# Early attention tasks in three lines with stores from ScalarE's queue, a reordered start of the output projection, and squares added in halves

## The chip, the cores and the metric

The kernel runs on one core of a Trainium2 chip. The metric is the device time of one execution, in microseconds (us); three runs of the kernel before gave 1561.88, 1563.29 and 1563.96, the median is 1563.29. The engines are named as in the profile: PE is the tensor engine, DVE VectorE, ACT ScalarE, POOL GpSimd, SP the engine that only issues DMAs here.

## The reference

One layer of a hybrid streaming encoder in fp32, on 1024 prompt rows and 32 sample rows (1056 columns in the kernel, where the activations lie transposed), with D_MODEL = 1024, eight heads of 64, a convolution branch of 512 channels and an MLP of 4096:

```python
h = rmsnorm(x, g_mix)
proj = h @ w_in                      # q, k, v, conv parts, two gates
y_attn = attend(q, k, v) @ w_attn_out
conv_out, new_buf = causal_conv(cc * cx, conv_buf, conv_w)
y_conv = (cb * conv_out) @ w_conv_out
merged = sigmoid(ga) * y_attn + sigmoid(gc) * y_conv
x = x + merged @ w_o
x = x + square(relu(rmsnorm(x, g_ffn) @ w_up)) @ w_down
x = x + sigmoid(rmsnorm(x, g_ple) @ w_ple_gate) * (p @ w_ple)
# attend: z = q k^T / 8, strictly causal;
# a = exp(log_sigmoid(z) + sum of log_sigmoid(-z) over the keys in between); out = a v
```

Outputs are the rms-normed rows, the keys and values, and the last rows of the convolution's input.

## The kernel before, in words

Every fp32 matmul is done as three matmuls on a high and a low part of each operand (a value is copied to a reduced type by ACT, and DVE subtracts that copy from the value for the low part). The large products are done as seven products of half-size blocks (Strassen-Winograd), with column quarters of 264; the halves and sums of blocks that this needs (B11, B21, B22, T1 to T4) are formed and split by ACT, DVE and POOL beside the matmuls.

The stages, with the times of the profile: the input projection to about 400 us; the attention loop to about 620; the branch products (`ps_oa`, `ps_oc`) to about 697; the output projection to about 780; up products to about 1120; down products to about 1448; then the per-layer embedding and the last norm.

**Attention.** 64 steps, each one tile of 128 queries of one head against all earlier keys. `ORDER` writes out what a step issues: the scores `z` (L864, L865) and their sigmoid `r` on ACT (L868; the score tile has one buffer, so PE's next `z` waits for the sigmoid before it), a running product by DVE (L882), turns of the weights by PE (`pa`, L918) with copies on ACT and DVE (L921, L922), and the weighted values `av` (L939). Between these, `fill` issues matmuls of other products in shares worked out ahead. SP's queue brings q, keys and values (L836 to L852), convolution data (L962) and weights. All engines work in order, so an instruction that waits holds whatever was issued behind it on its engine.

**The early tasks.** From step 3 on, one generator, `prior = ahead_all()`, is stepped once or twice per step (`1 + n % 2`, L1365). It does four gates and then eight weights one after the other. `ahead_gate` (L638) loads gate columns from `gd` (L640), three yields later scales them on DVE (`scaled`, L527), a yield later takes the sigmoid on ACT (L645) and stores to `gs_` (L646). `ahead_attn` (L627) loads a block of `w_attn_out` (L630), three yields later copies its high part on ACT (L633), takes the low part on DVE (L634) and stores both to `aod` (L635). Loads and stores all go through SP. The results are read back by the branch stage.

**The output projection.** `output_projection` (L1588) keeps a table of jobs, `at(q, f, ...)`: job f is issued at PE's unit q, a unit being 12 matmuls. The first jobs end the last branch output (`branch_post`, `merge_add`), form and split its halves (`merge_high` on ACT, `merge_low` on DVE, L1030 and L1034), sum them (`merge_sums`, L1054 to L1062) and split the parts T1 to T4 (`turn_part`, L1064, which also records at L1030 and L1034). `proj_high` (L1562) and `proj_low` (L1566) split the weights: `w0oA` (L1564) and `w1oA` (L1568). Results are added to `ceo` by DVE (L1682).

**The mean of squares.** `mean_squares` (L1716) is stepped once per unit in the up phase, from unit `SQ_AT` = 70 on. For each of eight tiles it loads (L1722), five yields later squares on ACT (L1725), a yield later adds on DVE (L1729); then three matmuls with ones (`ps_ms`, L1733) sum over the partitions. Meanwhile `mid_sums` (L1756) forms and stores the sums `m`, `ta`, `tb` of each set. Tiles come from one pool of 34 buffers.

Of the kernel before, what the change touches and what calls it, by code (L numbers as in the profile page):

```python
# [9 lines left out]
F32 = mybir.dt.float32  # L10
# [7 lines left out]
KD = D // P  # L18
# [25 lines left out]
CFILL = 4  # L44
ORDER = "LSAFBFG"
START = 2.5
SQ_AT = 70
MM = {mybir.EngineType.Activation, mybir.EngineType.PE, mybir.EngineType.DVE, mybir.EngineType.Pool}


# [1 line left out]
def tile_step(  # L52
# [574 lines left out]
    def ahead_attn(n):  # L627
        t = blk(f"ao{n}", F32R, [P, 2, 4, P])
        raw = t[:, 1].bitcast(F32)
        nc.sync.dma_start(raw, w_attn_out[n])  # L630
        for _ in range(3):
            yield
        nc.scalar.copy(t[:, 0], raw)  # L633
        dve(t[:, 1], raw, t[:, 0].bitcast(F32), op=sub)  # L634
        nc.sync.dma_start(aod[n], t.bitcast(F32).rearrange("p e k n -> p e (k n)"))  # L635
        yield

    def ahead_gate(n):  # L638
        m = blk(f"ga{n}")
        nc.sync.dma_start(m, gd[n])  # L640
        for _ in range(3):
            yield
        scaled(m)
        yield
        nc.scalar.activation(m, m, AF.Sigmoid)  # L645
        nc.sync.dma_start(gs_[n - 4], m)  # L646
        yield

    def ahead_all():
        for n in range(4, 8):  # L650
            yield from ahead_gate(n)
        for n in range(KD):
            yield from ahead_attn(n)

    def follow(nm, n, ms, wait=0):
        gens = []
# [366 lines left out]
    def merge_add(n, c):  # L1023
        dve(mg[n][:, c], mg[n][:, c], fetched["a", n][1][:, c], op=add)
# [111 lines left out]
    def branches():  # L1136

        seq = SEQ_B
        for i, b in enumerate(seq):
            prev, nxt = seq[i - 1] if i else None, seq[i + 1] if i + 1 < len(seq) else None  # L1140
            if i + 2 < len(seq):
                branch_fetch(seq[i + 2])
            else:
                row_fetch() if i + 2 == len(seq) else proj_fetch("A12", 1)
            done = prev and prev[0] == "a"
            if nxt:
                branch_high(nxt)
            else:
                row_high()
            branch_group(b, 0)  # L1150
            if prev:
                branch_post(prev, 2)
            if done:
                merge_add(prev[1], full[0])
                merge_high(prev[1])
            if nxt:
                if i:
                    branch_scale(nxt)
                branch_low(nxt)
                branch_sigmoid(nxt)  # L1160
            else:
                row_low()
                xload("ce", 0)
            if done:
                merge_low(prev[1])
                merge_sums(prev[1])
            for f in BESIDE.get(i, ()):
                f()
            branch_group(b, 1)
            branch_post(b, 0)  # L1170
            if nxt is None:
                merge_add(b[1], ts[0])
                proj_fetch("A12", 2)
            branch_group(b, 2)
            branch_post(b, 1)
            if nxt is None:
                merge_add(b[1], ts[1])
                merge_high(b[1], "1")
                merge_low(b[1], "1")
                proj_high("A12", 1)  # L1180
                proj_low("A12", 1)

    LK = PAST + DEC
    sampled = []
# [45 lines left out]
    with tc.manual_schedule(engines=MM):  # L1230
        nc.scalar.preload_act_table_set("sqrt_and_others")
        run(first_gates())
        for s_ in range(2, len(SETS)):
            nm, n = SETS[s_]
            if s_ == 2:
                side.append(after(1, stats_x()))
            elif s_ == 4:
                nc.scalar.preload_act_table_set("sigmoid_and_others")
            elif s_ == len(SETS) - 1:
                prior = ahead_all()  # L1240
            if s_ + 1 < len(SETS):
                side.append(prepare(f"i{s_ + 1}", AT_IN))
            else:
                side.extend([after(4, second_parts(0)), after(6, second_parts(1)), after(4, call(hooks_to, -20)), after(10, call(hooks_to, 0))])
            if s_ + 2 < len(SETS):
                side.append(after(5, call(fetch_in, s_ + 2)))
            m = blk(f"m1_i{s_}"), blk(f"m2_i{s_}")
            run(seven(f"i{s_}", *m, copy_of))
            if s_ + 1 < len(SETS):
                follow(nm, n, m, 6 * (s_ == 2))  # L1250
            else:
                last_m = n, m
        keys_values(0, 0)
        pools[:] = [gps]
        run(ahead(START))
        while side:
            run(range(1))
# [99 lines left out]
    with tc.manual_schedule(engines=MM):  # L1357
        queries(0, 0, 0)
        queries(0, 0, 1)
        for i, m in enumerate(last_m[1]):  # L1360
            nc.sync.dma_start(gd[last_m[0] + i], m)
        for n in range(LAST + 3):
            done_f, parts = 0, None
            if n > 2:
                for _ in range(1 + n % 2):  # L1365
                    next(prior, None)
            if n == 1:
                sample_loads()
            elif n == 3:
                sample_keys()  # L1370
            if n < LAST:
                i = steps[n][2]
                if i % 2 == 0 and n + 4 < LAST:
                    p_, j_, i_ = steps[n + 4]
                    queries(p_, j_, i_ // 2)
                if i == 2 and n + 8 < LAST:
                    keys_values(*steps[n + 8][:2])
            for op in ORDER:
                if op == "S" and n < LAST:
                    scores(*steps[n])  # L1380
                    if n == LAST - 1:
                        zf = zps.tile([P, 2, 512], F32, tag="z", name="zf")
                        spare_ps.extend(zf[:, h, :] for h in range(2))
                elif op == "L":
                    if 1 <= n <= LAST:
                        weigh(*steps[n - 1])
                    for f in pending + split_low:
                        f()
                    pending.clear()
                    split_low.clear()  # L1390
                elif op == "F" and n < LAST + 2:
                    done_f += 1
                    fill(share[n] + (share[n + 1] - share[n]) * done_f / nf)
                    if done_f == 1 and n in SAMPLE_AT:
                        next(sample, None)
                elif op == "G" and n >= 3 and steps[n - 3][2] % 2 == 1:
                    p, j, i_ = steps[n - 3]
                    gather(p, j, i_ // 2)
                elif op in "AB" and 2 <= n <= LAST + 1:
                    if op == "A":  # L1400
                        parts = flip(*steps[n - 2])
                    next(parts, None)
            for p, c in splits.get(n, ()):
                split_high(p, c)
            branches_ahead(n)
            if n == LAST + 1:
                fill(2 * total)
                hooks_to(len(plan))
                split_high(3, slice(0, 768))
        for f in pending + split_low:  # L1410
            f()
        split_high(3, slice(768, T))
        split_low.pop()()
# [174 lines left out]
    def output_projection():  # L1588
# [4 lines left out]
            jobs.setdefault(q, []).append(partial(f, *a))  # L1593

        last = KD - 1
        at(0, branch_post, ("a", last), 2)
        at(0, merge_add, last, ts[2])
        at(0, proj_fetch, "A12", 3)
        at(0, xload, "ce", 1)
        for j in (2, 3):  # L1600
# [7 lines left out]
        at(42, early_up, 1)  # L1608
        at(3, xload, "xb", 0)
        at(3, xload, "m2", 0)  # L1610
        at(1, merge_high, last, "2")
        for q, k, j in (
            (1, "T1", 0), (2, "T1", 1), (3, "T1", 2), (5, "T1", 3), (5, "T2", 0), (6, "T2", 1), (7, "T2", 2), (8, "T2", 3),
            (9, "T3", 0), (9, "T3", 1), (10, "T3", 2), (11, "T3", 3), (12, "T4", 0), (13, "T4", 1), (14, "T4", 2), (15, "T4", 3),
        ):
            at(q, turn_part, k, j)
        at(2, merge_low, last, "2")
        at(3, merge_sums, last, ("T3",))
        at(4, merge_sums, last, ("T2",))
        at(8, merge_sums, last, ("T4",))  # L1620
        for j in (1, 2, 3):
            q = AT["A11", j]
            for n in range(4):
# [92 lines left out]
    def mean_squares():  # L1716
# [3 lines left out]
        for n in range(KD):  # L1720
            r = blk(f"sq{n}")
            nc.sync.dma_start(r, xd[n])  # L1722
            for _ in range(5):
                yield
            nc.scalar.square(r, r)  # L1725
            yield
            ss = ss or r
            if n:
                dve(ss, ss, r, op=add)  # L1729
        rs2 = blk("rs2")  # L1730
        for c in ts:
            ps = tps.tile([P, 512], F32, tag="tp", name=f"ps_ms{c.start}")[:, :TT]
# [673 lines left out]
```

## Time and profile before

| | |
|---|---|
| median of three runs | 1563.29 us |
| the profiled execution | 1562.97 us |
| its span in the trace | 1561.2 us |
| PE busy | 1518.1 us, 97% of the span |
| DVE, ACT, POOL busy | 73%, 49%, 18% |
| mean granted clock of PE | 0.991 |
| bytes moved | 293.20 MB, 188 GB/s on the mean |

A row of a group gives line, engine, operation, output and inputs, the count and durations. A row of the timeline gives start and duration of one instruction, and in brackets the idle time of its engine before it and what released it. A row of waits gives who waited, for whom, the total, the number of times and the longest. PEclk is the share of its full clock that PE was granted. SPq and ACTq are the queues of DMA issues.

### The profile page before, as it was taken

The numbers are of one execution on the slowest core, as the hardware profiler recorded it, in microseconds if no ns is written. First come the engines' busy times: TensorE is split into PE (matmuls) and PEld (weight loads), VectorE is DVE, ScalarE is ACT, GpSimd is POOL, SyncE is SP. The second block draws the span as 40 slices with busy tenths as digits, with TensorE's granted clock in tenths as the row PEclk, the third lists the DMA queues.
The fourth block names the chain that finished last, engine by engine and source line by source line (L and its number), as shares of the span: only waits on it lengthen the run. The fifth ranks groups of instructions, "written<-read, shape, count | busy, mean of one in ns | idle before, by whom it ended". The sixth has DMA issues, their size and how long they took to land. (4 is left out here: it accounts for less than half of the span.)

```text
span 1561.2 us, 29913 instructions
## 1 busy us (share of the span) xinstructions
PE 1518.1 (97%) x11888; PEld 1501.3 (96%) x11888; DVE 1132.4 (73%) x1590; ACT 763.4 (49%) x1415; POOL 286.2 (18%) x318
## 2 busy tenths in 40 slices
PE   7999999999899899999999999999999999999997
PEld 7999999999798799999999999999999999999997
DVE  7568665667487788788876677755577995889756
ACT  6644444434466566224375555455644334444644
POOL 2223332221012222000001222222020130000253
PEclk9999999999999999999999999999999999999999
DMA  6513445414769852555754455443786897774443
GB/s 226 201 53 125 166 154 187 164 56 164 213 204 286 261 168 90 179 173 193 266 197 161 170 207 194 159 148 138 272 303 200 270 333 230 223 258 129 145 130 116
DMA packets 122765, 293.20 MB, mean 188 GB/s; under 512 B 14048, under 2 KB 34784, under 8 KB 122624
## 3 DMA queue, kind: packets, MB, share of 16 engines
q1 hardware_dynamic: 122336, 290.96, 55.6%
q8 instruction: 93, 1.52, 0.4%
q14 instruction: 48, 0.39, 0.1%
q10 hardware_dynamic: 288, 0.32, 0.1%
HBM read 204.15 MB, written 87.07 MB: 187 GB/s over the span
## 5 line engine op out<-in xcount | busy, mean ns | idle before, releaser
L1989 PE MATMUL ps_dn<-fh,whi_dn 128*128 128x264 f32 x896 | 255.0, 285 | 0.0
L1990 PE MATMUL ps_dn<-fl,whi_dn 128*128 128x264 f32 x896 | 254.8, 284 | 0.0
L1991 PE MATMUL ps_dn<-fh,wlo_dn 128*128 128x264 f32 x896 | 254.8, 284 | 0.0
L1991 PEld LDWEIGHTS ps_dn<-fh,wlo_dn 128*128 128x128 f32 x896 | 168.7, 188 | 0.1
L1990 PEld LDWEIGHTS ps_dn<-fl,whi_dn 128*128 128x128 f32 x896 | 168.6, 188 | 0.0
L1989 PEld LDWEIGHTS ps_dn<-fh,whi_dn 128*128 128x128 f32 x896 | 168.6, 188 | 0.0
L208 POOL TENSOR_TENSOR s_u<-raw_u,raw_u 128x512 f32<-128x512 f32 x22 | 32.7, 1487 | 367.2 <-DVE slS_u L169 317.0
L882 DVE TENSOR_TENSOR_SCAN r<-r 128x128 f32<-128x128 f32 (+3 forms) x64 | 86.6, 1353 | 3.4 <-POOL r L875 3.4
L208 POOL TENSOR_TENSOR s_i<-raw_i,raw_i 128x512 f32<-128x512 f32 x32 | 43.6, 1363 | 239.9 <-DVE slS_i L169 209.8
L1876 ACT CAST whi_dn<-raw_dn 128x1024 fp32r<-128x1024 f32 x40 | 42.0, 1050 | 83.0 <-PE ps_dn L1990 82.9
L1882 DVE TENSOR_TENSOR wlo_dn<-raw_dn,whi_dn 128x1024 fp32r<-128x1024 f32 x40 | 61.1, 1528 | 28.7 <-ACT whi_dn L1876 28.7
L241 PE MATMUL ps_A11i<-T,shS_i 128*128 128x264 f32 x256 | 73.1, 285 | 0.0
L875 POOL TENSOR_SCALAR_AFFINE_SELECT r<-r 128x128 f32<-128x128 f32 x64 | 35.4, 553 | 205.8 <-ACT r L868 198.2
L243 PE MATMUL ps_A11i<-T,slS_i 128*128 128x264 f32 x256 | 72.9, 285 | 0.0
L242 PE MATMUL ps_A11i<-T,shS_i 128*128 128x264 f32 x256 | 72.7, 284 | 0.0
L169 DVE TENSOR_TENSOR slS_i<-s_i,shS_i 128x512 fp32r<-128x512 f32 x48 | 34.9, 732 | 50.1 <-ACT shS_i L167 49.9
L1751 ACT ACTIVATE m<-m 128x528 f32<-128x528 f32 (+1 forms) x52 | 31.7, 610 | 80.2 <-DVE m L288 28.6
L1902 DVE TENSOR_TENSOR fl<-mr,fh 128x1056 fp32r<-128x1056 f32 x56 | 69.9, 1248 | 0.3 <-ACT q L1942 0.3
L922 DVE TENSOR_TENSOR at<-pa,at 128x512 fp32r<-128x512 f32 (+2 forms) x96 | 51.8, 549 | 22.4 <-ACT at L921 18.3
L2073 POOL TENSOR_TENSOR xx<-xx,pgs 128x384 f32<-128x384 f32 (+1 forms) x23 | 24.2, 1057 | 216.8 <-DVE pgs L2072 210.2
L1897 ACT CAST fh<-mr 128x1056 fp32r<-128x1056 f32 x56 | 60.0, 1072 | 0.2 <-issue 0.2
L169 DVE TENSOR_TENSOR slS_u<-s_u,shS_u 128x512 fp32r<-128x512 f32 x48 | 35.9, 747 | 33.1 <-ACT shS_u L167 33.1
(541 smaller groups left out, 5705.0 us busy)
## 6 DMA issues: line engine op xcount, KB each, us to landing
raw_dn<-in_w_down_dram SPq DMA_DIRECT2D x56, 512.0 KB, 4.8
raw_i<-in_w_in_dram SPq DMA_DIRECT2D x36, 512.0 KB, 4.4
mr<-mdT SPq DMA_DIRECT2D x32, 528.0 KB, 5.4
raw_u<-in_w_up_dram SPq DMA_DIRECT2D x32, 512.0 KB, 3.8
mr<-mdB SPq DMA_DIRECT2D x24, 528.0 KB, 6.3
mdB<-m SPq DMA_DIRECT2D x44, 264.0 KB, 2.7
raw_pg<-in_w_ple_gate_dram SPq DMA_DIRECT2D x17, 512.0 KB, 3.5
mdT<-ta SPq DMA_DIRECT2D x32, 264.0 KB, 2.1
```

Of the source, the lines that this page charges most:

```text
L169: dve(l, src, h.bitcast(F32), op=sub)
L208: f()
L241: nc.tensor.matmul(p_, wh[:, k, :], o[:, 0, c], start=new and n == 0, stop=False, **on)
L242: nc.tensor.matmul(p_, wh[:, k, :], o[:, 1, c], start=False, stop=False, **on)
L243: nc.tensor.matmul(p_, wl[:, k, :], o[:, 0, c], start=False, stop=z, **on)
L882: nc.vector.tensor_tensor_scan(rev, rev, rev, 1.0, ALU.mult, ALU.bypass)
L1882: dve(lo, raw, hi.bitcast(F32), op=sub)
L1897: nc.scalar.copy(h, mraw[v])
L1902: dve(l, mraw.pop(v), opd[v].bitcast(F32), op=sub)
L1989: nc.tensor.matmul(ps, hi[:, j, :], oh, start=j == 0, stop=False)
L1990: nc.tensor.matmul(ps, hi[:, j, :], ol, start=False, stop=False)
L1991: nc.tensor.matmul(ps, lo[:, j, :], oh, start=False, stop=j == NP_ - 1)
```

## The change

Three parts. First, the early tasks run in three lines, each stepped once per step of attention: weights 0 to 3, gates 4 to 7, weights 4 to 7, beginning at steps 3, 4 and 5. A load now comes five yields ahead of its use; the stores are issued by ACT, that of a weight two yields after its split. Second, in the table of the output projection, the parts of T1 come first and the last branch output later, and the weight split of the branch stage's end stands ahead of the halves. Third, the squares start at unit 40, each add is made in two halves of 528 columns with two yields ahead of each, and four yields follow the last.

```diff
-SQ_AT = 70
+SQ_AT = 40
...
     def ahead_attn(n):
...
         nc.sync.dma_start(raw, w_attn_out[n])
-        for _ in range(3):
+        for _ in range(5):
             yield
         nc.scalar.copy(t[:, 0], raw)
         dve(t[:, 1], raw, t[:, 0].bitcast(F32), op=sub)
-        nc.sync.dma_start(aod[n], t.bitcast(F32).rearrange("p e k n -> p e (k n)"))
+        yield
+        yield
+        nc.scalar.dma_start(aod[n], t.bitcast(F32).rearrange("p e k n -> p e (k n)"))
         yield
     def ahead_gate(n):
...
-        for _ in range(3):
+        for _ in range(5):
             yield
         scaled(m)
         yield
         nc.scalar.activation(m, m, AF.Sigmoid)
-        nc.sync.dma_start(gs_[n - 4], m)
-        yield
-
-    def ahead_all():
-        for n in range(4, 8):
-            yield from ahead_gate(n)
-        for n in range(KD):
-            yield from ahead_attn(n)
+        nc.scalar.dma_start(gs_[n - 4], m)
+        yield
+
+    def ahead_all(f, ns):
+        for n in ns:
+            yield from f(n)
...
                 merge_add(b[1], ts[1])
+                proj_high("A12", 1)
                 merge_high(b[1], "1")
+                proj_low("A12", 1)
                 merge_low(b[1], "1")
-                proj_high("A12", 1)
-                proj_low("A12", 1)
...
-                prior = ahead_all()
+                prior = [ahead_all(ahead_attn, (0, 1, 2, 3)), ahead_all(ahead_gate, (4, 5, 6, 7)), ahead_all(ahead_attn, (4, 5, 6, 7))]
...
             if n > 2:
-                for _ in range(1 + n % 2):
-                    next(prior, None)
+                for g in prior[: n - 2]:
+                    next(g, None)
...
-        at(0, branch_post, ("a", last), 2)
-        at(0, merge_add, last, ts[2])
+        at(2, branch_post, ("a", last), 2)
+        at(2, merge_add, last, ts[2])
...
-        at(1, merge_high, last, "2")
...
+            if (q, k, j) == (7, "T2", 1):
+                at(5, merge_high, last, "2")
+                at(5, merge_low, last, "2")
+                at(6, merge_sums, last, ("T3",))
+                at(7, merge_sums, last, ("T2",))
+            elif (k, j) == ("T4", 0):
+                at(12, merge_sums, last, ("T4",))
...
-        at(2, merge_low, last, "2")
-        at(3, merge_sums, last, ("T3",))
-        at(4, merge_sums, last, ("T2",))
-        at(8, merge_sums, last, ("T4",))
...
             nc.scalar.square(r, r)
-            yield
             ss = ss or r
-            if n:
-                dve(ss, ss, r, op=add)
+            for c in halves:
+                for _ in range(2):
+                    yield
+                if n:
+                    dve(ss[:, c], ss[:, c], r[:, c], op=add)
+        for _ in range(4):
+            yield
```

The table of units of `turn_part` changes with it: T1 from units 1, 2, 3, 5 to 0, 0, 1, 3; T2 from 5, 6, 7, 8 to 4, 7, 8, 8; T3 from 9, 9, 10, 11 to 9, 10, 10, 11; T4 stays.

SP's rows near the end of the early tasks, before: `ao7` is the last weight block, q the queries of the coming steps, raw_oc weights of the branch stage.

```order
L630 DMA ao7_6592<-in_w_attn_out_dram 128x512
L850 DMA q210_6618<-qd_166 64x2x256
L851 DMA q210_6618<-qd_166 64x256
L852 DMA q210_6618<-qd_166 64x256
L101 DMA raw_oc2_6837<-in_w_conv_out_dram 128x512
L101 DMA raw_oc3_7162<-in_w_conv_out_dram 128x512
L850 DMA q211_6696<-qd_166 64x2x256
L635 DMA aod_159<-ao7_6592 128x1024
L851 DMA q211_6696<-qd_166 64x256
L852 DMA q211_6696<-qd_166 64x256
```

The same load on SP now:

```order
L767 DMA gd_143<-sg2_5585 128x1056
L630 DMA ao7_6274<-in_w_attn_out_dram 128x512
L850 DMA q201_6312<-qd_166 64x2x256
L851 DMA q201_6312<-qd_166 64x256
L852 DMA q201_6312<-qd_166 64x256
L962 DMA cv20_6355<-cvd_169 128x1056
L962 DMA cv21_6357<-cvd_169 128x1056
```

The load of `ao7` stands ahead of q201 where it stood ahead of q210, three query tiles sooner, and no store `aod` stands between the parts of q211 on SP any more.

ACT's rows at the first gate's sigmoid (L645) before: `r` are the sigmoids of the scores, `at` copies of turned weights, `avl` and `sg` copies of results.

```order
L948 COPY avl000_5126<-av000_5120 64x256
L645 ACTIVATE ga4_5037<-ga4_5037 128x1056
L868 ACTIVATE r005_5138<-z005_5133 128x768
L921 CAST at00200_5078<-pa0030_5143 128x4x128
L868 ACTIVATE r006_5174<-z006_5169 128x896
```

The same gate's sigmoid on ACT now (L647):

```order
L921 CAST at00601_5277<-pa0074_5365 128x4x128
L637 DMA aod_159<-ao0_5037 128x1024
L647 ACTIVATE ga4_5063<-ga4_5063 128x1056
L648 DMA gs__158<-ga4_5063 128x1056
L633 CAST ao4_5130<-ao4_5130 128x512
L868 ACTIVATE r012_5390<-z012_5387 128x384
```

A store of a weight, the sigmoid, its store and another weight's copy now stand in a row ahead of the sigmoid r012, where one sigmoid stood ahead of r005.

DVE's rows at the start of the output projection, before: `w1oA` are low parts of the projection's weights, oB and oT low parts of its operands, `sa` and `mg` the last branch output, `ceo` sums of results.

```order
L1021 TENSOR_TENSOR sa7_8525<-ps_oa7_2_8672,sa7_8525 128x352
L1024 TENSOR_TENSOR mg7_8355<-mg7_8355,sa7_8525 128x352
L1682 TENSOR_TENSOR ceo0_8651<-ps_woA1100_8694,ceo0_8651 128x264
L1034 TENSOR_TENSOR oT10_8731<-sc0_5882,oT10_8731 128x528
L1682 TENSOR_TENSOR ceo0_8651<-ps_woA1101_8713,ceo0_8651 128x264
L1034 TENSOR_TENSOR oT11_8752<-sc2_6839,oT11_8752 128x528
L1034 TENSOR_TENSOR oB223_8729<-mg7_8355,oB223_8729 128x528
L1682 TENSOR_TENSOR ceo0_8651<-ps_woA1200_8735,ceo0_8651 128x264
L1034 TENSOR_TENSOR oT12_8774<-mg4_8030,oT12_8774 128x528
L1058 TENSOR_TENSOR mg6_8237<-mg7_8355,mg6_8237 128x528
L1682 TENSOR_TENSOR ceo0_8651<-ps_woA1201_8757,ceo0_8651 128x264
L1568 TENSOR_TENSOR w1oA122_8794<-raw_A12o2_8670,w0oA122_8792 128x512
```

The same stretch of DVE now, up to the same `w1oA122`; the first `w1oA121` stands right ahead of it, where oB213 and then `w1oA121` stood before.

```order
L1034 TENSOR_TENSOR oB213_8689<-mg7_8355,oB213_8689 128x528
L1034 TENSOR_TENSOR oT10_8710<-sc0_5889,oT10_8710 128x528
L1034 TENSOR_TENSOR oT11_8713<-sc2_6839,oT11_8713 128x528
L1684 TENSOR_TENSOR ceo0_8651<-ps_woA1100_8694,ceo0_8651 128x264
L1034 TENSOR_TENSOR oT12_8733<-mg4_8030,oT12_8733 128x528
L1684 TENSOR_TENSOR ceo0_8651<-ps_woA1101_8717,ceo0_8651 128x264
L1021 TENSOR_TENSOR sa7_8525<-ps_oa7_2_8672,sa7_8525 128x352
L1024 TENSOR_TENSOR mg7_8355<-mg7_8355,sa7_8525 128x352
L1684 TENSOR_TENSOR ceo0_8651<-ps_woA1200_8737,ceo0_8651 128x264
L1034 TENSOR_TENSOR oT13_8774<-mg6_8237,oT13_8774 128x528
L1684 TENSOR_TENSOR ceo0_8651<-ps_woA1201_8757,ceo0_8651 128x264
L1568 TENSOR_TENSOR w1oA122_8793<-raw_A12o2_8670,w0oA122_8791 128x512
```

The count of rows up to `w1oA122` is the same; the parts oT that take no late input moved up, the last branch output moved down, and oB223 and the sum at L1058 moved behind.

More of the change, by code (lines that the diff above doesn't have):

```diff
@@ L1610, in output_projection @@
         at(3, xload, "m2", 0)
-        at(1, merge_high, last, "2")
         for q, k, j in (
-            (1, "T1", 0), (2, "T1", 1), (3, "T1", 2), (5, "T1", 3), (5, "T2", 0), (6, "T2", 1), (7, "T2", 2), (8, "T2", 3),
-            (9, "T3", 0), (9, "T3", 1), (10, "T3", 2), (11, "T3", 3), (12, "T4", 0), (13, "T4", 1), (14, "T4", 2), (15, "T4", 3),
-        ):
+            (0, "T1", 0), (0, "T1", 1), (1, "T1", 2), (3, "T1", 3), (4, "T2", 0), (7, "T2", 1), (8, "T2", 2), (8, "T2", 3),
+            (9, "T3", 0), (10, "T3", 1), (10, "T3", 2), (11, "T3", 3), (12, "T4", 0), (13, "T4", 1), (14, "T4", 2), (15, "T4", 3),
+        ):
+            if (q, k, j) == (7, "T2", 1):
[5 more added lines that the diff above has]
+                at(12, merge_sums, last, ("T4",))
             at(q, turn_part, k, j)
-        at(2, merge_low, last, "2")
-        at(3, merge_sums, last, ("T3",))
-        at(4, merge_sums, last, ("T2",))
-        at(8, merge_sums, last, ("T4",))
         for j in (1, 2, 3):
@@ L1725, in mean_squares @@
             nc.scalar.square(r, r)
+            ss = ss or r
+            for c in halves:
[4 more added lines that the diff above has]
+        for _ in range(4):
             yield
-            ss = ss or r
-            if n:
-                dve(ss, ss, r, op=add)
         rs2 = blk("rs2")
```

## The prediction

> **What bounds the kernel now.** I read the page first, then the chain of waits of the tensor engine (PE), then the 140 us of attention stage by stage, then the other engines' waits there.
>
> ```profile
> span 1561.2 us, 29913 instructions
> PE 1518.1 (97%) x11888; PEld 1501.3 (96%) x11888; DVE 1132.4 (73%) x1590; ACT 763.4 (49%) x1415; POOL 286.2 (18%) x318
> ```
>
> PE is the bound: 1561.2 − 1518.1 = 43 us idle. The order of PE's matmuls hardly changes, so the change can win only these 43 us and what PE loses at a lower clock. PE's waits (total, times, longest) say where:
>
> ```profile
> PE z L864 <- ACT r L868: 14.4, 4, 6.1
> PE ps_woA L1710 <- DVE w1oA L1568: 2.5, 1, 2.5
> PE ps_ms L1733 <- DVE sq L1729: 2.2, 1, 2.2
> ```
>
> These three are the three edited places: scores in attention, the first tiles of the output projection, the mean of squares in the up phase. The stretches, with PE's busy time first and the granted clock (PEclk), DMA share and GB/s last:
>
> ```profile
> core 0: us, PE busy (x) PEld busy (x) DVE busy (x) ACT busy (x) POOL busy (x), PEclk, DMA share, GB/s
> 400.00:540.00 140.00, 122.26 (x923) 114.27 (x922) 103.73 (x140) 79.85 (x173) 26.57 (x79) 0.95 0.81 252
> 540.00:620.00 80.00, 78.36 (x574) 75.20 (x573) 68.23 (x101) 49.99 (x115) 18.39 (x50) 1.00 0.43 138
> 419.40:424.40 5.00, 4.98 (x21) 4.72 (x22) 3.33 (x5) 2.38 (x5) 0.87 (x4) 0.52 1.01 293
> 531.80:536.80 5.00, 4.91 (x18) 4.65 (x19) 4.80 (x7) 2.50 (x6) 2.67 (x4) 0.50 0.60 193
> 707.40:711.40 4.00, 3.90 (x19) 3.90 (x20) 4.00 (x9) 1.70 (x3) 0.00 (x0) 0.57 0.41 133
> 986.40:991.40 5.00, 4.92 (x25) 4.71 (x26) 1.58 (x4) 1.48 (x3) 0.00 (x0) 0.66 0.39 152
> ```
>
> While the early tasks run (400 to 540) PE idles 140 − 122.26 = 17.7 us; once they are over (540 to 620) it idles 1.6 in 80. The last four rows are what follows four of the stalls: the clock is down for 4 to 5 us. Loss of clock is length × (1 − PEclk): 5 × 0.48 = 2.4, 5 × 0.50 = 2.5, 4 × 0.43 = 1.7, 5 × 0.34 = 1.7 us.
>
> Why attention stalls shows in its last stall. On SP, ACT and PE in turn:
>
> ```profile
> 524.45 0.43 SPq L630 DMA_DIRECT2D ao<-in_w_attn_out_dram  x1
> ```
> ```profile
> 530.38 0.62 ACT L633 CAST ao<-ao 128x512 fp32r<-128x512 f32 x1 [5.15 <-DMA ao<-in_w_attn_out_dram]
> 531.02 0.81 ACT L868 ACTIVATE r<-z 128x768 f32<-128x768 f32 x1
> ```
> ```profile
> 531.89 0.74 PE L864 MATMUL z<-ks,q 128*128 128x448 f32 x1 [4.96 <-ACT r L868]
> ```
>
> SP issues the weight load at 524.45; ACT stands 5.15 us at the copy of that weight, with the sigmoid of a score tile queued behind it, and PE waits for that sigmoid. So PE waits for a load that PE has no need of yet. The load was late because SP was:
>
> ```profile
> SPq L635 <- DVE ao L634: 16.9, 8, 2.7
> SPq L646 <- ACT ga L645: 10.9, 3, 5.8
> SPq L635 <- DMA vv<-vd: 1.7, 2, 0.9
> SPq L850 <- DMA sc<-gd: 2.0, 1, 2.0
> SPq L850 <- PE pa L918: 30.8, 10, 6.0
> ```
> ```profile
> DMA to landing us min/median/max: 3.4/5.8/7.0
> ```
> ```profile
> DMA to landing us min/median/max: 4.8/5.2/7.5
> ```
>
> SP stood 27.8 us before the stores of the early tasks (first two rows), with later loads behind them. The last two answers are the landing times of the attention weights and of the gates. The 64 sigmoids of the scores give the length of a step of attention:
>
> ```profile
> L868 ACT ACTIVATE r<-z x64: 277/636/1028, 401.5 to 614.6; 128x128 f32<-128x128 f32 x8, 128x256 f32<-128x256 f32 x8, 128x384 f32<-128x384 f32 x8, 128x512 f32<-128x512 f32 x8
> ```
>
> That is 213 us for 63 steps; less the 22 us or so that the stalls take, 3.0 us a step on the mean. One line of tasks, stepped once or twice per step, gives a load of three yields about two steps, 6 us, less what SP stood.
>
> **Edit 1, early tasks.** Three lines, one yield each per step, five yields from load to use: 5 × 3.0 = 15 us against a worst landing of 7.5 and a worst stand of SP of 6.0 (its loads of q, behind PE) once the stores are gone from it. All four z waits and the waits behind the same stalls should go: at most 17.7 + 2.4 + 2.5 = 22.6 us. What stays: at the rate of 540 to 620, 140 × 1.64/80 = 2.9 us. What is added is ACT's work of issuing twelve stores:
>
> ```profile
> L633 ACT CAST ao<-ao x8: 617/621/653, 464.6 to 530.4; 128x512 fp32r<-128x512 f32 x8
> ```
> ```profile
> L645 ACT ACTIVATE ga<-ga x4: 1083/1084/1087, 417.4 to 454.9; 128x1056 f32<-128x1056 f32 x4
> ```
> ```profile
> L2176 ACTq DMA_DIRECT2D out_y_last_dram<-yl x1: 372/372/372, 1556.2 to 1556.2; - x1
> ```
>
> 12 × 0.37 = 4.5 us, hidden in ACT's 140 − 79.85 = 60 idle us unless it stands ahead of a sigmoid. The worst place is the step where a store, the first gate's sigmoid, its store and a copy come in a row: 0.37 + 1.08 + 0.37 + 0.62 = 2.4 us ahead of the next score's sigmoid, of a step of 3.0. Before, 1.08 us at most stood there. Between 0 and 2.4 us of PE; I take 1.5. DVE's work is the same, but 103.73 us have to fit into about 122 (85%, as in 540 to 620: 68.23 of 80), which is why I don't take all 17.7. Edit 1: 22.6 − 2.9 − 1.5 = 18.2 us. Its ends: 9 (half of the stalls return as DVE or ACT queueing) and 21.1 (only the idle of 2.9 less half stays).
>
> A store on ACT can also be held, as on SP: the third row above shows a store standing for a load it has nothing to do with (vv), and the fourth a load standing 2.0 us likewise. I take 2 us for all twelve together, between 0 and 12 × 0.9 = 10.8; the loads ahead of them are mostly two steps old.
>
> The Trainium skill, page "DMA: Bandwidth & Descriptors", section "Issuing engines are not separate DMA queues", speaks against this edit: queues of several engines share the same 16 DMA engines, and issuing from another one saves only the issue time. By that rule the move of the stores would save twelve issues of SP and no transfer time. It leaves out what the rows above show, that an issue which waits holds all behind it.
>
> **Edit 2, projection.** From DVE's row at the stall:
>
> ```profile
> 699.05 0.71 DVE L1034 TENSOR_TENSOR oB<-mg,oB 128x528 fp32r<-128x528 f32 x1 [0.75 <-ACT oB L1030]
> ...
> 702.64 0.71 DVE L1034 TENSOR_TENSOR oT<-sc,oT 128x528 fp32r<-128x528 f32 x1 [0.94 <-ACT oT L1030]
> ...
> 706.76 0.68 DVE L1568 TENSOR_TENSOR w1oA<-raw_A12o,w0oA 128x512 fp32r<-128x512 f32 x1
> ```
>
> PE wanted the second w1oA about 2.5 us before its end at 707.4, so at 704.9. Between the first and the second w1oA stand 11 DVE instructions before and 11 after, but other ones: B22 and a sum that nobody needs yet leave, the first oB, now behind the first w1oA, and a T1 part come in, and the parts that need no late input stand first, so the two idle pieces (0.75, 0.94) go, and with the first w1oA ahead of oB the second ends 0.75 + 0.94 + 0.6 (the pitch of oB) = 2.3 us sooner, near 705.1. A stall of 0.2 to 0.5 us stays, too short for the clock. Gain 2.5 + 1.7 − 0.5 = 3.7. What is moved back (B22 of the last third, the sums T3, T2, T4) has its cover in the units that PE works through before it wants them: counting DVE pieces of 0.4 to 0.7 us and PE units of 1.45, I estimate the third w1oA 0.4 us early, T2 2 and T3 4. If that cover is gone the stall is only moved, and the gain is 0.
>
> **Edit 3, squares.**
>
> ```profile
> 945.35 0.36 PE L241 MATMUL ps_S2u<-T,shA_u 128*128 128x264 f32 x1 [0.79 <-DVE m L295]
> 950.15 0.39 PE L243 MATMUL ps_A11u<-B,wlo_u 128*128 128x264 f32 x1 [0.75 <-DVE wlo_u L111]
> ```
> ```profile
> L1729 DVE TENSOR_TENSOR sq<-sq,sq x7: 1250/1258/2343, 928.8 to 985.2; 128x1056 f32<-128x1056 f32 x7
> ```
> ```profile
> 979.33 0.38 SPq L1722 DMA_DIRECT2D sq<-xd x1
> ```
> ```profile
> DMA to landing us min/median/max: 3.6/4.4/5.3
> ```
>
> The last load went out at 979.33, landing takes 4.4 and up to 5.3 us, square and add follow with 1.1 and 1.25, and the mean waited. The generator steps once per PE unit of 12 matmuls, which start 0.12 us apart:
>
> ```profile
> 412.89 0.28 PE L733 MATMUL ps_g<-B,whi_g 128*128 128x264 f32 x1
> 413.01 0.28 PE L734 MATMUL ps_g<-B,wlo_g 128*128 128x264 f32 x1
> ```
>
> So a unit is 1.45 us. The squares start 30 units earlier, but take 8 × 9 + 4 = 76 instead of 48, so the mean stays in its place (unit 116 after 118); what grows is the way from the last load to the mean, from 6 units (8.7 us) to 5 + 4 + 4 = 13 (18.9). The 2.2 and its clock, 1.7, go. Seven adds become fourteen halves of about 0.65 us, the longest DVE piece (2.34 us, beside GpSimd) half as long: the two waits above, 1.5 us, should go too. Against it: squares now run while the x sums of the first sets hold tile buffers, so one or two operands of a set wait for a buffer and store (2 us landing); I take 0.8, between 0 and 5.4 (everything won, lost again). Edit 3: 2.2 + 1.7 + 1.5 − 0.8 = 4.6 us.
>
> **Sum.** 18.2 − 2 + 3.7 + 4.6 = 24.5 us. The profiled execution took 1562.97 us, 1.8 more than its span and 0.3 less than the median of the runs, so the median should be 1563.3 − 24.5 = 1538.8; I say 1539.
>
> On the clock, the Trainium skill, page "TensorE: Matmul & The Clock Gate", Part 1, says that the clock halves after an idle window of about 3.4 us that runs freely, and as a practical rule asks for no gaps over about 3 us. The trace differs: gaps of 2.5 and 2.2 us were followed by 0.57 and 0.66. By that rule edits 2 and 3 would win 3.4 us less.
>
> **Rivals.**
>
> *Attention bound elsewhere.* The work that PE waited for is not less, only spread; if DVE (85%) and ACT now queue it up, half of edit 1 is lost: 1563.3 − 9 + 2 (the stores) − 8.3 (edits 2 and 3) = 1548. For it: DVE would be at 17.0 us per 20. Against it: 540 to 620 has the same DVE share with PE idle 1.6.
>
> *DMA bound.* DMA share 0.81 × 140 = 113 us of transfer must fit into about 120 (0.94). If the engines reach only 0.85, the stretch takes 133, edit 1 wins 7, and the time is 1563.3 − 7 − 8.3 = 1548. Against it: 419.40 to 424.40 shows 1.01.
>
> *Stores in ACT's queue, slower.* ACT works in order. If its stores stand for landings as SP's did, the sigmoid behind each comes late and PE with it, as at 531.89: 4.96 + 2.5 = 7.5 us a time. Three such waits eat the whole gain of 24.5, so from the fourth on it is slower: five make 1563.3 − 24.5 + 37.5 = 1576, four 1569. For it: twelve such places. Against it: a store follows its data by two steps or at once, and the longest stand of this sort in the rows is 2.0 us.
>
> *The change doesn't do what it says.* SP still stands for PE before q loads, and the loads may go out as late as now; only edits 2 and 3 win: 1555.
>
> **Chances.** Forecast (1531 to 1545) 0.65; attention or DMA bound (to 1553) 0.20; only small edits 0.07; within 0.2% 0.04; slower by the stores 0.04. About 0.2%, 3 us, is what a measurement of this kernel can tell from no change. The range: below, all bounds at their good end, 21.1 + 4.2 + 5.4 = 30.7 gives 1532.6, and I go to 1532; above, the two bound cases at 1548 with another 4 us for operands that wait, 1552.
>
> **What would show it.** Right: in 400 to 540 the z waits are gone, ACT no longer waits for ao loads, DVE not for ga, SP has no L635 and L646 stands, PEclk is 1.00, and the output projection begins 15 to 20 us earlier; ps_woA waits under 0.5 us; ps_ms doesn't wait. Wrong: ACT rows held at a store with PE z waiting behind; DVE above 95% over the whole stretch with PE idle; new waits of the up products for tb or sq tiles; ps_woA's wait back at a later tile. The forecast itself is wrong if edit 1 wins under 13 us.

## The result and the profile after

| | before | changed |
|---|---|---|
| median, runs of the first comparison | 1563.62 us (4 runs) | 1538.6 us (4 runs, 1538.17 to 1542.76) |
| ratio, 95% interval | | 0.9847 (0.9827 to 0.9866) |
| profiled execution, its span | 1562.97, 1561.2 us | 1542.76, 1541.0 us |
| a second profiled execution, its span | | 1538.01, 1536.3 us |
| mean granted clock of PE | 0.991 | 0.997 |

The kernel is 1.5% faster. The first profiled execution of the changed kernel was its longest run, 4 us above the three others; a second one (the run called e4_again below) is within 0.6 us of the median and is used for the comparison, and the first is used to see what the 4 us are.

The page of the first, and PE's waits in the second (total, times, longest):

```profile
span 1541.0 us, 29924 instructions
PE 1513.8 (98%) x11888; PEld 1497.4 (97%) x11888; DVE 1131.5 (73%) x1597; ACT 763.2 (50%) x1415; POOL 281.3 (18%) x318
```
```profile
PE ps_g L241 <- ACT B L385: 6.3, 1, 6.3
PE pa L918 <- DVE r L882: 3.4, 4, 1.2
PE av L939 <- DVE at L922: 1.4, 3, 0.7
PE z L864 <- ACT r L868: 0.8, 1, 0.8
```

The rows of ps_woA and ps_ms are gone, and z's 14.4 us are 0.8. What leads now is the kernel's start, which the change doesn't touch. The stretch of the early tasks in the second execution, with PE's busy time first and the granted clock third from the end; these 127 us hold 948 matmul records, where the 140 us from 400 to 540 held 923:

```profile
400.00:527.00 127.00, 120.90 (x948) 113.47 (x947) 106.10 (x145) 80.27 (x176) 23.56 (x80) 1.00 0.89 282
```

PE idles 6.1 us where it idled 17.7, at full clock. Where the time went, by the starts of the last score, of a product of the projection, and of the first and last S1 product of the up phase (from the groups of L864, L1710 or L1712, and L241):

```
                        before    changed, second execution    gained so far
last z                   614.0        598.4                        15.6
first ps_woA<-oT,s0oS    717.6        698.4                        19.2
first ps_S1u<-T,shS_u    809.1        789.6                        19.5
last ps_S1u<-B,shS_u    1117.1       1092.0                        25.1
span                    1561.2       1536.3                        24.9
```

The first z stood 0.9 us later than before, so attention gives 16.5, the way to the projection's products 3.6, and the up phase 5.6. The last of these leans on one profile of before: its up phase took 308.0 us, and that of the four kernels below that leave the squares alone (e1_attn, e2_proj, e10_stores, e11_far) 304.6 to 305.4. Against those, the 302.4 us of the second execution are a gain of 2.2 to 3.0.

### The profile page after: what moved, and what is told of

The parts are those of the page before. It is cut to its first block, busy times and chain, and to the rows that moved or that the text cites. A ratio compares the mean times of both kernels' runs of the same rounds, so it can differ in the third digit from the quotient of the medians.

```text
span 1541.0 us, 29924 instructions
## 1 busy us (share of the span) xinstructions
PE 1513.8 (98%) x11888; PEld 1497.4 (97%) x11888; DVE 1131.5 (73%) x1597; ACT 763.2 (50%) x1415; POOL 281.3 (18%) x318
## 5 line engine op out<-in xcount | busy, mean ns | idle before, releaser
L241 PE MATMUL ps_A11i<-T,shS_i 128*128 128x264 f32 x256 | 73.1, 285 | 0.1
L875 POOL TENSOR_SCALAR_AFFINE_SELECT r<-r 128x128 f32<-128x128 f32 x64 | 30.8, 481 | 195.3 <-ACT r L868 184.0
```

What stands on the lines that cost most here:

```text
L241: nc.tensor.matmul(p_, wh[:, k, :], o[:, 0, c], start=new and n == 0, stop=False, **on)
```

## The experiments

Ratios are to the kernel before, run beside each on the same chip; its median there was 1561.7 to 1562.2 us, over 1558.5 to 1566.6, a wider spread than the changed kernel's. The kernels of one table share their runs of the kernel before; those of the last table ran on another chip than the rest. The code shown is a few lines of each edit.

**One part at a time.** e1_attn has the first edit alone, e2_proj the second, e3_sq the third:

```diff
 e1_attn
+                prior = [ahead_all(ahead_attn, (0, 1, 2, 3)), ahead_all(ahead_gate, (4, 5, 6, 7)), ahead_all(ahead_attn, (4, 5, 6, 7))]
+        nc.scalar.dma_start(aod[n], t.bitcast(F32).rearrange("p e k n -> p e (k n)"))
 e2_proj
+        at(2, branch_post, ("a", last), 2)
+                at(5, merge_high, last, "2")
 e3_sq
+SQ_AT = 40
+            for c in halves:
```

> Only the early tasks are changed (three lines, far loads, stores on ScalarE's queue); projection and squares are as before. Theory (three separate stalls, whose gains add up): 16 to 18 us less than before, near 1546; the stalls at the second w1oA (2.5 us) and at ps_ms (2.2 us) stay. Rival (part of what attention wins is given back later, because work that comes sooner finds its loads not there): 12 us or less, with new waits of PE in the branches or the projection.

> Only the order of the projection's first work is changed. Theory: 3.5 to 4.2 us less than before, near 1559.5, from the 2.5 us wait and the 1.7 us at the low clock behind it. Rival (the stall is only moved to a later tile): within 1 us of before.

> Only the squares are changed (from unit 40, adds in halves). Theory: 4 to 5 us less than before, near 1559, from the 2.2 us wait, 1.7 us at the low clock and the waits of 0.3 to 0.8 us beside the long adds, less 1 us of new waits around the first units. Rival (the earlier start takes tile buffers from the up sets and gives it all back): within 1 us of before.

> The changed kernel as it is, for a second profile. Its first profiled execution took 1542.8 us and its other runs 1538.2 to 1538.7. Theory (the 4 us are one stand of ScalarE at a store in front of a sigmoid, 3.4 us, with the low clock behind it, which depends on how the transfers fall): in an execution near 1538.5 this stand is under 2 us and PEclk stays at 1.00 from 400 to 540. Rival (they lie elsewhere or are spread over the whole span): the stand is there in an execution near 1538.5 too.

Measured:

| | median us | ratio | interval |
|---|---|---|---|
| e1_attn | 1542.31 | 0.9873 | 0.9857 to 0.9889 |
| e2_proj | 1558.63 | 0.9980 | 0.9971 to 0.9989 |
| e3_sq | 1558.11 | 0.9974 | 0.9963 to 0.9984 |
| e4_again | 1538.50 | 0.9850 | 0.9834 to 0.9866 |

All three gain by themselves: 19.8, 3.1 and 4.1 us by the ratios, 27.0 together against 23.4 for the whole. Each has an uncertainty of 1.4 to 2.5 us, so the sum of three and the whole do not contradict each other. e1_attn won more than expected, and not all of it is attention: from the first z to the last it takes 195.9 us where before took 212.9, a gain of 17.0, and another 3.4 come in the up phase (304.6 against 308.0), which it doesn't edit. The third edit claims the same stretch, so these microseconds may stand twice in the sum of three. PE's rows show part of them:

```profile
690.89 0.44 PE L1710 MATMUL ps_woA<-oB,w1oA 128*128 128x264 f32 x1 [2.17 <-DVE w1oA L1568]
968.00 0.86 PE L1733 MATMUL ps_ms<-sq,ones 128*128 128x352 f32 x2 [1.69 <-DVE sq L1729]
```

The two stalls that this kernel leaves alone are there, but here the second has no low clock behind it. These are the stretches behind the two, then e2_proj behind its 2.2 us stall at ps_ms, and e3_sq behind its 2.5 us stall at w1oA:

```profile
690.90:694.90 4.00, 4.00 (x20) 4.00 (x21) 4.00 (x9) 1.70 (x3) 0.00 (x0) 0.57 0.40 133
968.00:973.00 5.00, 5.00 (x35) 4.57 (x36) 2.58 (x6) 1.94 (x4) 0.00 (x0) 1.00 0.44 148
```
```profile
985.00:990.00 5.00, 5.00 (x35) 4.58 (x36) 2.56 (x6) 2.17 (x4) 0.00 (x0) 1.00 0.35 136
```
```profile
707.60:711.60 4.00, 3.98 (x31) 3.82 (x32) 4.00 (x9) 1.71 (x3) 0.00 (x0) 1.00 0.41 133
```

The clock at the same two places was 0.57 and 0.66 in the profile of before. So the 1.7 us of low clock behind a stall of 1.7 to 2.5 us is there in some executions and not in others; the forecast counted it as certain, twice. The last section shows on what it depends. In e2_proj the wait for the second w1oA is down to what was forecast:

```profile
708.59 0.39 PE L1712 MATMUL ps_woA<-oB,w1oA 128*128 128x264 f32 x1 [0.20 <-DVE w1oA L1568]
```

**The 4 us of the first profiled execution.** ACT in the first profiled execution, and in the second:

```profile
516.05 0.34 ACTq L637 DMA_DIRECT2D aod<-ao  x1
516.49 0.70 ACT L868 ACTIVATE r<-z 128x640 f32<-128x640 f32 x1 [3.41 <-DMA q<-qd]
```
```profile
515.09 0.33 ACTq L637 DMA_DIRECT2D aod<-ao  x1
515.52 0.70 ACT L868 ACTIVATE r<-z 128x640 f32<-128x640 f32 x1 [2.53 <-PE av L939]
```

In both, ACT stands at the store of a weight with the next sigmoid behind it. The release was a load of q, which has nothing to do with the stored tile; the second row names PE, but the trace's semaphore records show the same load there too (last section). PE's rows, and the stretch behind the first:

```profile
517.25 0.44 PE L864 MATMUL z<-ks,q 128*128 128x384 f32 x1 [1.74 <-ACT r L868]
```
```profile
517.20:522.20 5.00, 4.95 (x22) 4.73 (x23) 4.57 (x5) 2.82 (x7) 0.88 (x4) 0.66 0.92 283
```
```profile
516.28 0.44 PE L864 MATMUL z<-ks,q 128*128 128x384 f32 x1 [0.85 <-ACT r L868]
```

1.74 us and 5 × 0.34 = 1.7 us of clock in the one, 0.85 us in the other: 2.6 us of the 4.7 between the two spans. The first execution also has a second stand, 2.07 us of ACT at the store of a gate (497.93), with 0.92 us of a z wait behind it, and its up phase is 1.5 us longer, with the two waits for wlo_u (1.0 us) that the second lacks. The expected bound for the stand, under 2 us, was missed (2.53), the full clock was met. So somewhat more than half of the difference is this stand, the rival of other places has a part, and the stand is there in good runs too. That made the queue of the stores the next question.

**What in the first edit does the work?** Four kernels take its three ingredients apart: the three lines, the five yields, and ScalarE's queue.

```diff
 e5_sp, from the changed kernel
-        nc.scalar.dma_start(aod[n], ...)        # and the same for gs_
+        nc.sync.dma_start(aod[n], ...)
 e10_stores, from the kernel before
-        nc.sync.dma_start(aod[n], ...)          # and the same for gs_
+        nc.scalar.dma_start(aod[n], ...)
 e11_far, from the kernel before
-        for _ in range(3):                      # both loads
+        for _ in range(5):
 e7_three, from the changed kernel
-        for _ in range(5):                      # both loads
+        for _ in range(3):
```

> The changed kernel with the twelve stores back on SP; lines and five yields stay. Theory (what counts is that a load has about 15 us before its use; a stand of SP of some 6 us then does no harm, and ScalarE no longer stands at a store in front of a sigmoid): as fast as the changed kernel or up to 3 us faster, ratio to before 0.983 to 0.986, no wait of PE for a sigmoid over 1 us. Rival (the queue of the stores is what frees the loads): at least 5 us slower than the changed kernel, ratio 0.988 or more, SP again standing over 10 us at the stores and ScalarE or VectorE waiting for loads.

> The kernel before with only the issue of the twelve stores moved to ScalarE's queue; one line, three yields, stores right behind their data. Theory: loads no longer stand behind stores on SP (27.8 us of stands go) and a part of the stalls goes, but two steps are still short of a landing of 5 to 7 us: 4 to 12 us less than before. Rival (moving issues to another engine saves only the issue time, some 4 us of an SP that is not on the path): within 3 us of before. Rival (a store on ScalarE right behind VectorE's subtraction holds the sigmoids behind it): 3 us or more above before.

> The kernel before with only the five yields instead of three between load and use; one line, stores on SP. Theory (distance is what counts): over 3 steps, 10 us, less SP's stands: 8 to 15 us less than before. Rival (the stores on SP hold the loads whatever their place): under 5 us less.

> The changed kernel with three yields between load and use instead of five; three lines, stores on ScalarE. Theory: three steps are 9 us against landings up to 7.5, so most waits stay hidden and the time is within 4 us of the changed kernel, ratio 0.985 to 0.988. Rival (five are needed): ScalarE or VectorE wait for early loads again, over 5 us in all, and the time is 5 us or more above the changed kernel.

Measured:

| | median us | ratio | interval |
|---|---|---|---|
| e5_sp | 1535.09 | 0.9831 | 0.9816 to 0.9846 |
| e10_stores | 1565.59 | 1.0027 | 1.0016 to 1.0037 |
| e11_far | 1547.28 | 0.9907 | 0.9894 to 0.9921 |
| e7_three | 1534.01 | 0.9825 | 0.9810 to 0.9840 |

Moving the stores alone makes the kernel slower by 4.2 us (2.5 to 5.8), and moving them back makes the changed kernel 3.4 us faster by the medians; the intervals of the two ratios overlap, the runs don't (1533.93 to 1535.82 against 1538.01 to 1538.93). ACT's queue is no part of the gain. In e5_sp one z wait of 1.7 us is left, for a load of q itself, and no stand of ACT at a store; SP stands 8.7 us in all before the stores, against 30.2 in the kernel before, counted the same way, and this does no harm. The profiles don't show the 3.4 us at the stores, though: from the first z to the last, e5_sp takes 196.1 us and the second execution of the changed kernel 196.4. The first execution, with its longer stands, took 199.3. e10_stores shows both sides; ACT's waits, then SP's, then PE's:

```profile
ACT ao L633 <- DMA ao<-in_w_attn_out_dram: 8.7, 4, 4.5
ACT r L868 <- DVE ao L634: 4.8, 4, 1.3
```
```profile
SPq L962 <- DMA aod<-ao: 9.5, 3, 3.7
SPq L850 <- DMA aod<-ao: 2.5, 1, 2.5
SPq L851 <- DMA aod<-ao: 2.5, 1, 2.5
```
```profile
PE z L864 <- ACT r L868: 19.2, 8, 6.9
```

SP no longer stands at its own stores, but it stands 14.5 us before loads until a store that ACT issued has landed, ACT still waits 8.7 us for the weights, and now sigmoids also wait for the subtraction that a store needs. PE's z waits rise from 4 to 8.

e11_far, with only a longer way from load to use, wins 14.5 us: all z waits are gone, and from the first z to the last it takes 201.0 us, 11.9 less than before. A wait of ps_oc comes in, at 554, where the tasks of this kernel, still one line, reach further into the loop:

```profile
PE ps_oc L1092 <- DVE sc L1096: 2.9, 1, 2.9
PE pa L918 <- DVE r L882: 2.7, 4, 1.3
```

Distance is the cause, as the forecast had it; three lines with three yields give it as well. In the rows, the eight weight loads have 5.8 to 8.8 us from issue to use in the kernel before, where the slowest takes 7.0 us to land, 6.3 to 18.5 in e11_far, 5.8 to 13.3 in e7_three and 10.9 to 23.3 in the changed kernel. That the tasks are spread thinner, as they are in e11_far, isn't what counts: e7_three issues the loads of all twelve tasks within 62 us (408.7 to 470.8), before within 116 (408.6 to 524.4). e7_three needs no fifth yield, since its only wait for an early load is 1.1 us of ACT, and is 4.5 us faster than the changed kernel, 2.8 of them between the first z and the last (193.6 us). In PE's waits of e7_three no z stands at all, and pa's 3.4 are 1.7:

```profile
PE pa L918 <- DVE r L882: 1.7, 4, 0.6
PE av L939 <- DVE at L922: 1.5, 3, 0.7
```

The two extra steps set which early task falls into which step. With five yields a gate's scaling of 1.25 us stands ahead of the running product `r` on DVE at two places where PE waits 1.19 and 1.18 us for it; with three the tasks fall elsewhere. That is read from the rows, and no run moved one task alone. In e7_three no store stands on ACT, either.

**Best of both, and the squares.**

```diff
 e9_sp3, from the changed kernel: both undone
-        for _ in range(5):
+        for _ in range(3):
-        nc.scalar.dma_start(aod[n], ...)
+        nc.sync.dma_start(aod[n], ...)
 e8_pool, from the changed kernel
-        nc.scalar.dma_start(aod[n], ...)        # and the same for gs_
+        nc.gpsimd.dma_start(aod[n], ...)
 e6_sq40whole, from the changed kernel
-            for c in halves:
-                for _ in range(2):
-                    yield
-                if n:
-                    dve(ss[:, c], ss[:, c], r[:, c], op=add)
+            for _ in range(4):
+                yield
+            if n:
+                dve(ss, ss, r, op=add)
 e14_sq70, from the changed kernel
-SQ_AT = 40
+SQ_AT = 70
```

> The changed kernel with three yields instead of five and the stores back on SP: only the three lines, and the two yields ahead of a weight's store, are left of the first edit. Theory (three lines make the distance, and both the fifth yield and ScalarE's queue are needless): ratio 0.981 to 0.983, 0 to 1.5 us faster than either of the two undone alone (1534.0 and 1535.1). Rival (each of the two covers for the other: three steps hold only where SP is free of stores): stalls at early loads return, and it is 3 us or more slower than the changed kernel, ratio 0.987 or more.

> The changed kernel with the twelve stores issued by GpSimd. Theory (ScalarE's order is what the stores hurt; GpSimd has little to do there): as with the stores on SP, ratio 0.982 to 0.985, and no stand of ScalarE ahead of a sigmoid. Rival (GpSimd's selections of the scores, which VectorE waits for, stand behind the stores there as the sigmoids did): ratio 0.986 or more, with VectorE waiting for GpSimd over 5 us more.

> The changed kernel with each add of the squares in one piece again, the start at unit 40 and the nine units for each tile kept. Theory (the long adds cost waits of their own): ps_ms doesn't wait, but waits of 0.5 to 0.8 us behind a long add are back, and it is 0.5 to 2 us slower than the changed kernel, ratio 0.985 to 0.987. Rival (only the place of the mean counts): within 0.5 us of the changed kernel.

> The changed kernel with the squares from unit 70 on again, adds in halves, so that the mean comes some 30 units later than in it. Theory (what helps ps_ms is the longer way from the last load to the mean, not the early start): the same time as the changed kernel within 1 us, ps_ms not waiting. Rival (the mean is needed where it stood): new waits of PE behind the mean, 1 us or more slower. Rival (the early start takes buffers of the up sets): the waits of 0.2 to 0.7 us of the first up units go, and it is 1 us faster.

Measured:

| | median us | ratio | interval |
|---|---|---|---|
| e9_sp3 | 1533.51 | 0.9818 | 0.9804 to 0.9831 |
| e8_pool | 1535.09 | 0.9828 | 0.9815 to 0.9842 |
| e6_sq40whole | 1537.23 | 0.9841 | 0.9827 to 0.9854 |
| e14_sq70 | 1538.25 | 0.9848 | 0.9835 to 0.9862 |

e9_sp3, with only the three lines and the deferral left of the first edit, is the fastest kernel here, 5 us under the changed one (4 runs each, 1533.08 to 1534.36 against 1538.01 to 1538.93) and beats both kernels; it can't be told from e7_three. So the two costs, 3.4 us of the stores and 4.5 of the yields, don't add up: with three yields it no longer matters who issues the stores. Between the first z and the last, the two extra yields cost the same with either queue, 2.8 us on ACT and 2.7 on SP (193.4 us here, 196.1 in e5_sp). PE's waits of it:

```profile
PE pa L918 <- DVE r L882: 1.9, 4, 0.7
PE av L939 <- DVE at L922: 1.5, 3, 0.7
```

e8_pool is as fast as e5_sp: what hurts is the store's place in ACT's order, not the store. That it does so by way of the sigmoid behind it is seen in the two stands above and not shown for the whole 3.4 us. Waits of DVE for GpSimd are 3.4 us as before.

e6_sq40whole is not slower but 1.3 us faster than the changed kernel by the medians; the runs of e4_again lie 0.9 us apart, and the ratios' intervals overlap, so whole adds cost nothing that can be seen here. The waits behind wlo_u that the halves were to remove come and go with halves: 1.0 us in the first profile of the changed kernel, none in the second, 0.8 in e14_sq70. PE's waits of e6_sq40whole, then of that first profile:

```profile
PE ps_A11u L243 <- DVE wlo_u L111: 1.1, 2, 0.6
```
```profile
PE ps_A11u L243 <- DVE wlo_u L111: 1.0, 2, 0.7
```

e14_sq70 is the changed kernel's equal, and neither has a ps_ms row. What is left of the third edit as a cause is the way from the last load to the mean; no run lengthens that way alone. Before, the mean stood 7.2 us behind the last load's 979.33, and in the second execution the two are 22.7 us apart; the mean before, then load and mean now:

```profile
986.48 0.86 PE L1733 MATMUL ps_ms<-sq,ones 128*128 128x352 f32 x2 [2.18 <-DVE sq L1729]
```

```profile
937.39 0.32 SPq L1724 DMA_DIRECT2D sq<-xd  x1
```
```profile
960.09 0.75 PE L1739 MATMUL ps_ms<-sq,ones 128*128 128x352 f32 x2
```

## Why the prediction was right, and which steps were not

The time (1538.6 us measured, 1539 forecast) and the three places were right. By its terms, measured in the second execution's stages and by single edits:

| term | forecast | stage | edit alone |
|---|---|---|---|
| attention, stores taken off | 16.2 | 16.5 | 19.8 (17.3 to 22.3) |
| projection | 3.7 | 3.6 | 3.1 (1.7 to 4.5) |
| squares | 4.6 | 5.6 (2.2 to 3.0 against four other profiles) | 4.1 (2.5 to 5.8) |

That the squares' term came out so near is in part luck: 1.5 us of it stood for halves and 1.7 for a low clock, and neither is sure, as said below. The 19.8 of attention alone hold 3.4 us of the up phase.

- *z waits end because loads are further ahead.* Right, and shown by e11_far: distance alone wins 14.5 us and leaves no z wait.
- *SP's stands at the stores hold the loads, so their queue matters.* This step failed. Moved alone, the stores cost 4.2 us (e10_stores); back on SP, 3.4 us are won (e5_sp). With the stores moved, SP stands elsewhere, before loads and for landings. The sum survived because it counted no gain for the move itself, and a cost of 2 us for the stores, which measured 3.4 with five yields and 0.5, too little to tell, with three (e7_three against e9_sp3). The Trainium skill, "DMA: Bandwidth & Descriptors", section "Issuing engines are not separate DMA queues", said that another issuing engine saves only issue time; the runs agree, and add that the issuing engine's own order is what it costs.
- *Slower rival, stores in ACT's queue.* Its mechanism is real, 3.41 and 2.53 us of stand, but at one place that reaches PE, two in the first execution, and not four; each cost PE 0.85 to 1.74 us and not 4.96.
- *Five yields give 15 us against a landing of 7.5.* True (10.9 us at least in the rows), but the cover was more than needed: three do (e7_three). The two extra yields cost 2.7 to 2.8 us between the first z and the last, part of the residual that the forecast put down as 2.9 + 1.5.
- *Rivals of a bound elsewhere.* Not seen: DMA share rose to 0.89 in the squeezed stretch and PE stayed busy.
- *A residual stall at the second w1oA of 0.2 to 0.5 us.* Right: 0.20 in e2_proj, no wait in the whole change. The later parts had their cover.
- *Clock behind the short stalls, 1.7 us twice, counted as certain.* Mis-sized: it comes in some executions only, by where the stall falls in the clock's windows. For attention, where stalls were 5 to 6 us, low clock stood behind them in each profile that has them.
- *Halves of the adds remove 1.5 us.* Failed: whole adds are as fast (e6_sq40whole). A half takes 0.70 us, but the longest add is still 1.79 us. The up phase of before's profile is long by some 3 us against four others with the same squares, so the 1.5 us may need no cause of their own.
- *The early start is paid with 0.8 us of waits for buffers.* Not seen: PE waits for no buffer. Its waits of 0.2 us or more in the up phase of the second execution are 0.29 and 0.22 us near 899, for split parts; without the early start other short ones come, and the time is the same (e14_sq70).

## What to carry to other kernels

When PE waits for an engine that waits for a load it has no hurry for, put distance between load and use: more lines in flight do it, and each extra step beyond that may only shift work into a worse place. An issue of a DMA that may have to wait belongs on an engine with nothing urgent behind it. Count what a stall costs in clock as a chance, not as a term, when it is about 2 us long. Before a stage's gain is put down to an edit, look how much that stage differs between profiles of kernels that leave it alone: 3 us here.

## What the runs showed of the hardware that was not expected

PE's clock fell to 0.66 over 5 us behind a stall of 1.74 us and stayed at 1.00 behind one of 2.5 us; behind the 2.5 us stall at the second w1oA it did the one in before and the other in e3_sq, two kernels that are alike up to there. The difference lies in the stall's place. Within an execution the falls stand whole multiples of 3.41 us apart: in that of before, at 417.37, 530.01, 707.51 and 987.40 us, 33, 52 and 82 times 3.41 from one to the next. Laid on this grid, the window that holds the stall and the one behind it, in before and then in e3_sq:

```profile
704.09:707.51 3.42, 0.96 (x9) 0.75 (x8) 3.42 (x8) 2.76 (x6) 0.00 (x0) 1.00 0.58 230
707.51:710.92 3.41, 3.41 (x15) 3.41 (x16) 3.41 (x7) 1.70 (x3) 0.00 (x0) 0.50 0.48 156
```
```profile
703.59:707.00 3.41, 1.58 (x13) 1.37 (x12) 3.41 (x8) 3.39 (x7) 0.00 (x0) 1.00 0.76 294
707.00:710.41 3.41, 2.79 (x22) 2.79 (x23) 3.41 (x7) 1.71 (x3) 0.00 (x0) 1.00 0.48 157
```

In before the whole stall lies in one window: PE idles 2.46 us of it, and the next window has half the clock. In e3_sq, whose falls at 416.87 and 529.51 give the grid, a window's end cuts the stall, which leaves 1.83 us on one side, and the clock stays. Over all profiles here, from 30 to 1500 us, a window at full clock in which PE idled 2.17 us or more was always followed by half the clock, 14 times, and one with 1.70 us or less never; between them lie this 1.83, which wasn't, and the 1.74 of the first profile of the changed kernel, which was. The Trainium skill, "TensorE: Matmul & The Clock Gate", Part 1, speaks of a window of about 3.4 us that runs freely, which fits the grid; its practical rule (section "Why this matters for your kernels") of no gaps over about 3 us is not safe by these rows.

A DMA issue can stand for a transfer that touches none of its data: a store of a weight on ACT 3.41 us for a load of q, and loads on SP 14.5 us in all for stores that ACT had issued. The trace's semaphore records say what ties them, and it is how this program is built: all 806 DMAs of SP and ACT share eight completion semaphores in rotation, and in the profiles of before and of the changed kernel none of the 798 that come later on a semaphore was issued until the one before it there had landed. The store at 516.05 uses the semaphore of the load of q issued at 507.15, which landed at 515.98; in the second execution the pair is 515.09 and 506.35, landed at 515.02. In e10_stores each load that stood uses the semaphore of the store that it stood for.
